# Two image stores cut by channels into uneven pieces, and TensorE's opening put into a loop of one turn, in a Winograd-style 3x3 convolution

## The chip, the cores and the metric

The kernel runs on one core of a Trainium2 chip. The metric is the device time of one execution in microseconds (us); the time before is the median of three runs. The engines are TensorE (PE in the profile, its weight loads PEld), VectorE (DVE), ScalarE (ACT), GpSimd (POOL) and SyncE (SP). Sixteen DMA engines move data between device memory (HBM) and the on-chip memory SBUF. SP, ACT and POOL each issue transfers into a queue of their own (q1, q10 and q0 in the profile, in this order); the sixteen engines serve all three.

## What is computed

A 3x3 convolution with padding of one over 16 images of 64 channels and 64x64 pixels, into 128 output channels, in float32:

```python
batch, c_in, h, w, c_out = 16, 64, 64, 64, 128
x_pad = np.pad(x, ((0, 0), (0, 0), (1, 1), (1, 1)), mode='constant')
...
output[b, co] += weight[co, ci, kh, kw] * x_pad[b, ci, kh:kh+h, kw:kw+w]
```

## The kernel before

**Tiling.** Two images make a pair p (0 to 7): 2 x 64 input channels fill the 128 partitions, so a pair is loaded as one tile of 128 partitions x 64 rows x 64 columns of float32 (2 MB). An output image is one such tile too, with the 128 output channels on the partitions. Eleven such tiles, `homes`, hold inputs and outputs in turn; `IN_HOME` and `OUT_HOME` (L18, L19) say which pair and which image of a pair (b2 = 0 or 1) use which home. A pair is worked on in four blocks of 16 rows, so there are 32 blocks n in all.

**Compute.** For a block, ScalarE casts input rows to fp16 (`cast`, L106), GpSimd adds neighbouring rows (`sums`, L100), TensorE makes three groups of products in PSUM banks (L287), ScalarE copies the first group out of PSUM (L194), and VectorE adds it to the other two into even and odd rows of the output home (L227). TensorE's main loop (L256) has eight turns, one for each pair. Ahead of it stands TensorE's head (L243 to L255): it waits for a tile of zeros, runs seven idle products (`spin(7)`), waits for the weights, transposes them with 18 products, runs four more idle products and gives three credits.

**Transfers.** SP loads the weights, pair 0 in two halves and pairs 1 to 3 (L138 to L142); GpSimd's queue loads pairs 4 to 7 as homes come free (L168, L182). A finished image is stored whole: image b2 = 0 of each pair by SP (L143 to L147), image b2 = 1 by ScalarE's queue (L204 to L209), after VectorE's count for the pair's last block. The last pair alone is stored in two halves of 32 rows. In program counting the pairs start at 0, so the change's "pairs 6 and 7" are p = 5 and p = 6. A store adds 16 to a semaphore: one of its own where the home is used again, else `s_end`. Both (p 5, b2 0) in home 8 and (p 6, b2 0) in home 1 are the last use of their home, so they count on `s_end`. At the end SP waits for 16 times `n_end`, the number of those stores (L299).

**Order.** Every engine's program is written out by hand in issue order; only TensorE loops. A store on SP waits for nothing but VectorE's count, and SP has no other work. The queue of one DMA engine is served in order within SP's, ACT's and POOL's share.

Of the kernel before, what the change touches and what calls it, by code (L numbers as in the profile page):

```python
# [11 lines left out]
H = W = 64  # L12
CO = 128
TILES = 6
G0, G21, G1, G01, G2 = range(5)


IN_HOME = [0, 1, 2, 3, 4, 0, 10, 6]  # L18
OUT_HOME = [(5, 6), (7, 8), (1, 9), (2, 5), (3, 7), (8, 4), (1, 9), (2, 5)]  # L19
CUTS = [(0, 18), (18, 34), (34, 50), (50, 64)]  # L20


def kernel(tc: tile.TileContext, x: bass.AP, weight: bass.AP, out: bass.AP):
    nc = tc.nc
# [3 lines left out]
    def sem(name):  # L28
        return tc.alloc_semaphore(name)

    def sbuf(name, shape, dt):
        return nc.alloc_sbuf_tensor(name, shape, dt).ap()


    s_w, s_pool = sem("s_w"), sem("s_pool")
    s_in = [sem(f"s_in{p}") for p in range(NP)]
    s_in0b = sem("s_in0b")
    s_pe = sem("s_pe")
    s_act = sem("s_act")
    s_dve = sem("s_dve")  # L40
    s_out = {}
    s_end, s_done = sem("s_end"), sem("s_done")
# [14 lines left out]
    PE, ACT, DVE, POOL, SP = nc.tensor, nc.scalar, nc.vector, nc.gpsimd, nc.sync  # L57
# [4 lines left out]
    def free(home):  # L62
        if home not in user:
            return None
        kind, arg = user[home]
        return (s_pe, consumed(arg)) if kind == "in" else (arg, 16)
# [4 lines left out]
    with tc.tile_critical(sync_engine=EngineType.Pool):  # L71
        homes = [sbuf(f"home{k}", [128, H, W], F32) for k in range(11)]
# [4 lines left out]
        w16 = sbuf("w16", [CO, 64 * 9], F16)  # L77
        Wt = sbuf("Wt", [128, 5, 3, CO], F16)
        zeros = sbuf("zeros", [128, 512], F16)
        ident = sbuf("ident", [128, 128], F16)  # L80
        banks = [nc.alloc_psum_tensor(f"bank{k}", [128, RB, W], F32).ap() for k in range(8)]
        flat = [b.rearrange("p j c -> p (j c)") for b in banks]
# [4 lines left out]
        def rows(t):  # L87
            return t.rearrange("p (j i) c -> p j i c", i=2)
# [4 lines left out]
            ).then_inc(s or s_in[p], 16)  # L93

        def store(eng, p, b2, lo, hi, s):
            return eng.dma_start(
                out[2 * p + b2, :, lo:hi, :], homes[OUT_HOME[p][b2]][:, lo:hi, :]
            ).then_inc(s, 16)

        def sums(eng, lo, n, p):  # L100
            v = rows(homes[IN_HOME[p]])
# [4 lines left out]
        def cast(m):  # L106
            lo, hi = CUTS[m % NB]
            return ACT.copy(xs[:, lo:hi, :], homes[IN_HOME[m // NB]][:, lo:hi, :])  # L108
# [3 lines left out]
        pieces, n_end = {}, 0  # L112
        last_user = {}
        for p in range(NP):
            for b2 in range(2):
                last_user[OUT_HOME[p][b2]] = (p, b2)
        for p in range(5):
            user[IN_HOME[p]] = ("in", p)
        for p in range(NP):
            for b2 in range(2):  # L120
                h = OUT_HOME[p][b2]
                gate_out[p, b2] = free(h)
                if last_user[h] == (p, b2):
                    s = s_end
                else:
                    s = s_out[p, b2] = sem(f"s_out{p}{b2}")
                cuts = [(3, 0, H)] if p < NP - 1 else [(1, 0, 32), (3, 32, H)]
                for blk, lo, hi in cuts:
                    pieces[p, b2, blk] = (lo, hi, s)
                    n_end += s is s_end  # L130
                user[h] = ("out", s)
            if p + 5 < NP and p in (0, 1, 2):
                q = p + 5
                gate_in[q] = free(IN_HOME[q])
                user[IN_HOME[q]] = ("in", q)
# [7 lines left out]
        for p in range(NP):  # L143
            for blk in range(NB):
                if (p, 0, blk) in pieces:
                    SP.wait_ge(s_dve, adds(NB * p + blk, 2))
                    store(SP, p, 0, *pieces[p, 0, blk])  # L147
# [5 lines left out]
                out=ident,  # L153
# [17 lines left out]
        for k in range(2, 2 * NP):  # L171
            p = k // 2
# [5 lines left out]
            if k in (4, 6, 8):  # L178
                q = k // 2 + 3
# [5 lines left out]
        wp_bank = {G1: 4, G2: 5, G0: 6}  # L185
# [5 lines left out]
        for n in range(NB * NP):  # L191
            for b2 in range(2):
                when(
                    ACT.copy(uts[n % 2][b2], banks[(6 * n + b2) % 8]), s_pe, tiles(n, 1 + b2)  # L194
                ).then_inc(s_act, 1)
            m = n + 1
            if m < NB * NP:
                if m % NB == 0:
                    ACT.wait_ge(s_in[m // NB], 16)
                if m == 1:  # L200
                    ACT.wait_ge(s_in0b, 16)
                cast(m).then_inc(c_cast, 1)
            done = n - 1
            if done >= 0 and (done // NB, 1, done % NB) in pieces:  # L204
                p = done // NB
                ACT.wait_ge(s_dve, adds(n, 1))
                store(ACT, p, 1, *pieces[p, 1, done % NB])
        ACT.wait_ge(s_dve, adds(NB * NP, 1))
        store(ACT, NP - 1, 1, *pieces[NP - 1, 1, NB - 1])  # L209


# [5 lines left out]
        for n in range(NB * NP):  # L217
            p, blk = divmod(n, NB)
            j0 = RB * blk
            for i in range(2):  # L220
                for b2 in range(2):
                    if blk == 0 and i == 0 and gate_out[p, b2] is not None:
                        DVE.wait_ge(*gate_out[p, b2])
                    if i == 0 and b2 == 0:
                        DVE.wait_ge(s_act, copies(n, 2))
                    add = when(
                        DVE.tensor_add(  # L227
                            rows(homes[OUT_HOME[p][b2]])[:, j0 : j0 + RB, i, :],
                            banks[(6 * n + 2 + 2 * i + b2) % 8],
# [9 lines left out]
        def spin(n):  # L239
            for _ in range(n):  # L240
                PE.matmul(flat[7], zeros[:, 0:128], zeros)  # L241

        PE.wait_ge(s_dve, 1)  # L243
        spin(7)
        PE.wait_ge(s_pool, 3)
        for kh, g in ((1, G1), (2, G2), (0, G0)):
            for k in range(3):
                t = 3 * kh + k
                for q in (0, 64):
                    mm = PE.matmul(  # L250
                        flat[wp_bank[g]][q : q + 64, k * CO : k * CO + CO], w16[:, t::9], ident
                    )
            mm.then_inc(s_pe, 1)
        spin(4)
        PE.sem_inc(c_bank, 3)  # L255
        with nc.Fori(0, NP, engines=(EngineType.PE,), hint_back_edge=True):  # L256
            for blk in range(NB):
# [6 lines left out]
                for gi, (taps, credits) in enumerate(groups):  # L264
# [5 lines left out]
                    for wi, off in taps:  # L270
                        for kw in (1, 0, 2):
                            c_lo, c_hi = max(0, 1 - kw), min(W, W + 1 - kw)
                            for b2 in range(2):
                                p0 = 64 * b2
                                lo, hi = j0, j0 + RB
# [3 lines left out]
                                else:  # L279
# [7 lines left out]
                                mm = PE.matmul(  # L287
                                    acc[b2][:, lo - j0 : hi - j0, c_lo:c_hi],
                                    Wt[p0 : p0 + 64, wi, kw, :],
                                    rhs,  # L290
                                    start=i == 0,
                                    stop=i == n - 1,
                                )
# [36 lines left out]
```

## Time and profile before

| what | us |
|---|---|
| median of 3 runs (128.70 to 128.82) | 128.75 |
| time of the profiled execution | 129.4 |
| span of the profiled execution, first to last instruction | 126.8 |
| VectorE's last add ends (the last work of any compute engine) | 111.7 |
| last store issued | 111.7 |
| SP's wait for the last stores | 14.0 |

The span leaves 2.6 us of the profiled execution's time outside it. The page's strips have 40 slices of 3.17 us each. Its transfers: 17.07 MB read from HBM and 33.55 MB written. Besides its views, the trace keeps one record for each DMA packet (queue, bytes, start, duration) but not the number of the DMA engine that moved it. A packet is one channel's rows of one image or pair: 16,384 bytes for 64 rows, 8,192 for 32.

### The profile page before, as it was taken

Reading aid. Unit: us, or ns where it says so; the run is one execution under the profiler, and the core shown is the slowest. Engines: PE = TensorE matmul, PEld = TensorE weight load, DVE = VectorE, ACT = ScalarE, POOL = GpSimd, SP = SyncE. Lnnn points to the kernel's source line nnn. Section 1 sums busy time; section 2 is a strip of 40 time slices with the busy share of each in tenths; the row PEclk is TensorE's granted clock in tenths of the full one; section 3 lists DMA queues with packets and bytes.
Section 4 is the critical chain, followed back from the end, with each engine's and each line's share of the span. In section 5 each row is a group of like instructions: output and inputs, shape, how many; then the busy total and the mean of one; then the engine's idle time right before and its main releaser. Section 6 shows DMA issues by size and latency. Waiting matters only on the chain.

```text
span 126.8 us, 2528 instructions
## 1 busy us (share of the span) xinstructions
PE 108.3 (85%) x989; PEld 57.2 (45%) x989; DVE 84.1 (66%) x133; ACT 67.2 (53%) x100; POOL 39.1 (31%) x26
## 2 busy tenths in 40 slices
PE   5979999999999999999999999999999999800000
PEld 2535555555555555555555555555555555300000
DVE  0058887888788778777877787778777877720000
ACT  4366656665666566656665666566656666300000
POOL 2218455271517161706060606070707000000000
PEclk9999999999999999999999999999999999997555
DMA  4999999999999999999999999999999999999930
GB/s 125 384 442 450 429 419 424 439 289 413 419 434 450 429 411 424 439 444 419 424 426 444 434 419 419 439 439 429 419 434 429 442 419 419 429 416 434 424 145 13
DMA packets 4035, 50.65 MB, mean 399 GB/s; under 512 B 448, under 2 KB 448, under 8 KB 576
## 3 DMA queue, kind: packets, MB, share of 16 engines
q1 hardware_dynamic: 2160, 25.46, 48.5%
q10 hardware_dynamic: 1296, 16.78, 31.0%
q0 software_dynamic: 576, 8.39, 15.5%
q14 instruction: 3, 0.02, 0.0%
HBM read 17.07 MB, written 33.55 MB: 399 GB/s over the span
## 4 chain that ended last, share of the span: by engine, by line
PE 80%; DVE 1%; DVEq 0%; issue 0%
PE bank L287 80%; DVE home L227 1%; DVEq L71 0%
## 5 line engine op out<-in xcount | busy, mean ns | idle before, releaser
L227 DVE TENSOR_TENSOR home<-bank,ut 128x512 f32<-128x512 f32 x128 | 81.9, 686 | 21.8 <-PE bank L287 21.6
L287 PE MATMUL bank<-xs,Wt 64*128 64x504 f16 (+3 forms) x768 | 87.5, 373 | 0.0
L287 PEld LDWEIGHTS bank<-xs,Wt 64*128 64x128 f16 x768 | 43.9, 94 | 38.2
L194 ACT COPY ut<-bank 128x512 f32<-128x512 f32 x64 | 34.4, 589 | 37.8 <-PE bank L287 37.8
L102 POOL TENSOR_TENSOR ss<-home 128x1024 f16<-128x1024 f32 x15 | 35.5, 2367 | 50.7 <-PE bank L287 48.4
L108 ACT CAST xs<-home 128x1024 f16<-128x1024 f32 (+2 forms) x32 | 33.8, 1058 | 0.0
L287 PE MATMUL bank<-ss,Wt 64*128 64x504 f16 (+1 forms) x192 | 26.5, 377 | 0.7 <-PEq L266 0.7
L287 PEld LDWEIGHTS bank<-ss,Wt 64*128 64x128 f16 x192 | 10.9, 94 | 10.4 <-issue 1.2
L241 PE MATMUL bank<-zeros 128*128 128x512 f16 x11 | 4.5, 567 | 1.4 <-DVE zeros L212 1.4
L91 POOL DMA_DIRECT2D home<-in_x_dram x4 | 2.4, 600 | 4.8 <-DMA home<-in_x_dram 4.8
L213 DVE TENSOR_TENSOR Wt<-Wt 128x384 f16<-128x384 f16 x1 | 0.4, 359 | 4.7 <-ACT Wt L188 4.7
L188 ACT CAST Wt<-bank 128x384 f16<-128x384 f32 x3 | 1.2, 487 | 3.0 <-PE bank L250 3.0
L241 PEld LDWEIGHTS bank<-zeros 128*128 128x128 f16 x11 | 1.3, 131 | 3.3 <-issue 1.7
L188 ACT ACT_TABLE_LOAD x1 | 1.3, 1283 | 0.9 <-PEq L314 0.9
L250 PEld LDWEIGHTS bank<-ident,w 128*64 128x64 f16 x18 | 1.1, 209 | 0.8 <-POOL w L164 0.8
L164 POOL CAST w<-w_raw 128x576 f16<-128x576 f32 x1 | 0.7, 662 | 2.2 <-DMA w_raw<-in_weight_dram 2.2
L250 PE MATMUL bank<-ident,w 128*64 128x128 f16 x18 | 1.3, 327 | 0.0
L102 DVE TENSOR_TENSOR ss<-home 128x512 f16<-128x512 f32 x2 | 1.3, 686 | 0.0
L212 DVE MEMSET zeros<- 128x256 uint32 x1 | 0.3, 272 | 1.1 <-PEq L314 1.1
L214 DVE TENSOR_TENSOR Wt<-Wt 128x384 f16<-128x384 f16 x1 | 0.4, 358 | 0.0
L150 POOL MEMSET ident<- 128x128 f16 x1 | 0.2, 204 | 0.5 <-POOLq L71 0.5
L152 POOL TENSOR_SCALAR_AFFINE_SELECT ident<-ident 128x128 f16<-128x128 f16 x1 | 0.3, 292 | 0.1
(4 smaller groups left out, 0.4 us busy)
## 6 DMA issues: line engine op xcount, KB each, us to landing
out_dram<-home SPq DMA_DIRECT2D x7, 2048.0 KB, 24.1
out_dram<-home ACTq DMA_DIRECT2D x7, 2048.0 KB, 20.3
home<-in_x_dram POOLq DMA_DIRECT2D x4, 2048.0 KB, 20.5
home<-in_x_dram SPq DMA_DIRECT2D x3, 2048.0 KB, 20.8
home<-in_x_dram SPq DMA_DIRECT2D x2, 1024.0 KB, 6.1
out_dram<-home SPq DMA_DIRECT2D x2, 1024.0 KB, 11.7
out_dram<-home ACTq DMA_DIRECT2D x2, 1024.0 KB, 14.0
w_raw<-in_weight_dram SPq DMA_DIRECT2D x1, 288.0 KB, 2.8
```

The source lines that it names most:

```text
L91: return eng.dma_start(homes[IN_HOME[p]][:, lo:hi, :], x_rows[128 * p : 128 * p + 128, lo:hi, :]).then_inc(s or s_in[p], 16)
L102: return eng.tensor_add(ss[:, lo : lo + n, :], v[:, lo : lo + n, 0, :], v[:, lo : lo + n, 1, :])
L108: return ACT.copy(xs[:, lo:hi, :], homes[IN_HOME[m // NB]][:, lo:hi, :])
L164: when(POOL.tensor_copy(w16, w_raw), s_w, 16).then_inc(s_pool, 1)
L188: ACT.copy(wrow(g), flat[wp_bank[g]][:, 0 : 3 * CO]), s_pe, i + 1
L194: ACT.copy(uts[n % 2][b2], banks[(6 * n + b2) % 8]), s_pe, tiles(n, 1 + b2)
L213: when(DVE.tensor_sub(wrow(G21), wrow(G2), wrow(G1)), s_act, 2)
L214: when(DVE.tensor_sub(wrow(G01), wrow(G0), wrow(G1)), s_act, 3)
L227: DVE.tensor_add(rows(homes[OUT_HOME[p][b2]])[:, j0 : j0 + RB, i, :], banks[(6 * n + 2 + 2 * i + b2) % 8], uts[n % 2][b2],),
L241: PE.matmul(flat[7], zeros[:, 0:128], zeros)
L250: mm = PE.matmul(flat[wp_bank[g]][q : q + 64, k * CO : k * CO + CO], w16[:, t::9], ident)
L287: mm = PE.matmul(acc[b2][:, lo - j0 : hi - j0, c_lo:c_hi], Wt[p0 : p0 + 64, wi, kw, :], rhs, start=i == 0, stop=i == n - 1,)
```

## The change

Two things. First, for image 0 of pairs p = 5 and p = 6 SP's one store of 128 channels x 64 rows becomes three: rows 0 to 31 of all channels, then rows 32 to 63 of 120 channels, then rows 32 to 63 of the other eight. The eight are the last ones for p = 5 and the first ones for p = 6. `n_end` counts the added stores. Second, TensorE's head is put, unchanged, into a loop of one turn whose first instruction is placed at slot 0 of a block of instruction fetch; a branch in front of it skips the slots between.

```diff
+PARTS = {
+    (5, 0): [(0, CO, 0, 32), (0, 120, 32, H), (120, CO, 32, H)],
+    (6, 0): [(0, CO, 0, 32), (8, CO, 32, H), (0, 8, 32, H)],
+}
...
         def store(eng, p, b2, lo, hi, s):
-            return eng.dma_start(
-                out[2 * p + b2, :, lo:hi, :], homes[OUT_HOME[p][b2]][:, lo:hi, :]
-            ).then_inc(s, 16)
+            for c0, c1, r0, r1 in PARTS.get((p, b2), [(0, CO, lo, hi)]):
+                eng.dma_start(
+                    out[2 * p + b2, c0:c1, r0:r1, :],
+                    homes[OUT_HOME[p][b2]][c0:c1, r0:r1, :],
+                ).then_inc(s, 16)
...
-                    n_end += s is s_end
+                    if s is s_end:
+                        n_end += len(PARTS.get((p, b2), [0]))
...
-        PE.wait_ge(s_dve, 1)
-        spin(7)
+        with nc.Fori(0, 1, engines=(EngineType.PE,), head_slot={EngineType.PE: 0}):
+            PE.wait_ge(s_dve, 1)
+            spin(7)
...
```

The rest of the head, down to `spin(4)`, moves into the loop with no other edit.

More of the change, by code (lines that the diff above doesn't have):

```diff
@@ L241, in spin @@
                 PE.matmul(flat[7], zeros[:, 0:128], zeros)
-        PE.wait_ge(s_dve, 1)
-        spin(7)
[L245 to L254, printed above, removed]
+        with nc.Fori(0, 1, engines=(EngineType.PE,), head_slot={EngineType.PE: 0}):
+            PE.wait_ge(s_dve, 1)
+            spin(7)
+            PE.wait_ge(s_pool, 3)
+            for kh, g in ((1, G1), (2, G2), (0, G0)):
+                for k in range(3):
+                    t = 3 * kh + k
+                    for q in (0, 64):
+                        mm = PE.matmul(
+                            flat[wp_bank[g]][q : q + 64, k * CO : k * CO + CO], w16[:, t::9], ident
+                        )
+                mm.then_inc(s_pe, 1)
+            spin(4)
         PE.sem_inc(c_bank, 3)
```

## The prediction

> **What bounds the kernel now.** I read the page's strips first, then the chain of waits, then SP's own waits, then the DMA share in short windows at the end.
>
> ```profile
> PE   5979999999999999999999999999999999800000
> PEclk9999999999999999999999999999999999997555
> DMA  4999999999999999999999999999999999999930
> GB/s 125 384 442 450 429 419 424 439 289 413 419 434 450 429 411 424 439 444 419 424 426 444 434 419 419 439 439 429 419 434 429 442 419 419 429 416 434 424 145 13
> ```
>
> The DMA strip is full from the second slice to slice 38 and outlives PE's by four slices. The chain of waits stops where compute ends, and SP's waits show what comes after.
>
> ```profile
> 7.74 101.44 PE bank L287 x948
> 109.18 1.90 DVE home L227 x3
> 111.08 0.60 DVEq L71
> ...
> SPq L299 <- DMA out_dram<-home: 14.0, 1, 14.0
> ```
>
> Compute ends at 111.7; SP then waits 14.0 us (L299) for the last stores. So the transfers set the end. The windows show that it is not all sixteen DMA engines:
>
> ```profile
> 120.00:121.00 1.00, 0.00 (x0) 0.00 (x0) 0.00 (x0) 0.00 (x0) 0.00 (x0) 0.50 1.05 442
> 121.00:122.00 1.00, 0.00 (x0) 0.00 (x0) 0.00 (x0) 0.00 (x0) 0.00 (x0) 0.50 0.43 180
> 122.00:123.00 1.00, 0.00 (x0) 0.00 (x0) 0.00 (x0) 0.00 (x0) 0.00 (x0) 0.50 0.08 33
> 123.00:124.00 1.00, 0.00 (x0) 0.00 (x0) 0.00 (x0) 0.00 (x0) 0.00 (x0) 0.50 0.06 25
> 124.00:125.00 1.00, 0.00 (x0) 0.00 (x0) 0.00 (x0) 0.00 (x0) 0.00 (x0) 0.50 0.08 33
> 125.00:126.80 1.80, 0.00 (x0) 0.00 (x0) 0.00 (x0) 0.00 (x0) 0.00 (x0) 0.50 0.00 0
> ```
>
> The last two columns are the DMA share and GB/s. A share of 1/16 = 0.0625 is one engine: from about 122.3 to 125.3 a single DMA engine works while fifteen stand idle. The packet records (queue, bytes, start and end) say the same to the packet. Each engine's last packet of the two final stores ends between 121.25 and 121.61 on twelve engines, then at 121.91, 121.94, 122.35, and on the last at 125.26; the last landing is at 125.71.
>
> Why is one engine late? A 16,384-byte packet takes 611 ns almost everywhere. One unbroken sequence, each packet starting where the one before ends, does not:
>
> ```
> q10 16384  91.061-91.723  662
> q1  16384  91.720-92.373  653
> q10 16384  92.370-93.014  644
> q1  16384  93.010-93.654  644
> ```
>
> It runs from 28.8 to 113.6, about 130 packets with some 4.0 us over 611 ns in sum, loads among them. Before (9 to 24 us: compute and loads, no stores) no packet exceeds 611; after 113.6 (stores, no compute) its 8,192-byte packets take 309 like the others'. It starts each packet without a gap, so it can finish earlier only if it is given fewer bytes.
>
> **The change, part by part.** *Channels to engines.* A 128-channel store puts 16 completion records, one for each engine, behind 128 data packets: eight packets an engine. The trace shows no 120-channel transfer. Bounds: at eight packets an engine, as now, 120 channels occupy fifteen engines and one is left out; or all sixteen share it and nobody is spared. I take the first as nearest to the rows: one engine then loses eight packets in each of the two images, 16 in all. [...]
>
> *What the spared engine saves.* The last 8,192-byte packets start 0.306 us apart, so 16 x 0.306 = 4.90 us. If it is the late engine it ends at 125.26 - 4.90 = 120.4, and is no longer last.
>
> *What the others pay.* The two eight-channel pieces are 16 packets. At one an engine, eight engines get two more: 2 x 0.306 = 0.61 us (bounds: 0 if the last ones are not among them, and 4.90 if one engine takes all 16). Halving packets costs 2 x 309 - 611 = 7 ns for each of 16 packets, 0.11 us, and a few completion records of 9 ns. So the fifteen end at latest at 122.35 + 0.61 + 0.11 = 123.07, or at 122.46 if the one at 122.35 gets nothing more.
>
> *Conflicts at the source.* In the 128-channel stores each engine reads at 309 ns per 8,192 bytes. Whether fifteen engines reading 120 channels get in each other's way is not in the trace. Bounds: 0, and two engines sharing one path, twice the time: 16 x 0.309 = 4.94 us on every engine. I take 0.3 us, near the lower end: the only slowing seen once transfers run steadily is that late engine's, about 30 ns in 611, and 5% of 4.94 is 0.25.
>
> *SP's added issues.* Four more at 0.332 us. SP issues at 85.5, 98.3 and 104.7 and is idle between, so two more cost 0.66 us of idle time; no one queues behind. Landings here take 10.6 to 29.0 us, the DMA queues being full, so they are hidden; were the queues empty, the later pieces would land up to 0.66 us late, which no step waits for before the end.
>
> *TensorE's head.* It adds a skip to a new fetch block, a register step and a branch, and no product. The nearest rows are PE's 0.7 us behind its sequencer ahead of the main loop, 1.4 us behind the first zeros, and instruction packets of 309 to 436 ns. Bounds: -0.7 to +2 us on the start of the main loop. The loop is 101.4 us with no idle time, so the delay arrives whole at 111.7, and there it is covered by the queue: the last stores, issued at 111.1 and 111.7, would land in about the 6.1 us of the opening 1024-KB loads, at 117.8, if the engines were free, but these are busy to 121.3 at least. That is 3.5 us of cover, and behind the change still some 3 us. Moving it past would cost one for one. I take 0 for the end.
>
> **Sum.** Profiled execution: last packet from 125.26 to between 122.46 and 123.07, a gain of 2.2 to 2.8; less 0.3 for conflicts, 1.9 to 2.5, middle 2.2. From 129.4 this is 127.2. The median of the timed runs is 0.65 lower than the profiled execution: 128.75 - 2.2 = 126.55, say 126.6. Its own range: 125.8 (2.8 and 0.15 of spread) to 128.4 (conflicts of 2 us).
>
> **The rivals.** *Source conflicts decide (slower).* Two engines that read through one path in both 120-channel pieces: 16 packets at 618 instead of 309. The fifteen end at 122.46 + 4.94 = 127.4 or up to 128.0, so 128.75 + 2.1 to 2.7, about 131.1. It breaks even when the extra reaches 2.5 us, that is, when a packet of these pieces averages about 465 ns. For it: the order of channels on engines may change with 120. Against it: loads and stores from two queues mix freely at 611. [...] Chance 0.15.
>
> *Another engine is spared (the change doesn't do what it says).* The late engine keeps its bytes; it ends at 125.26, plus 0.11, plus 0.61 if it is one of the eight: 128.85 to 129.5. The records carry no engine number, which is all that speaks for it. [...] Chance 0.15.
>
> *The lateness belongs to the profiled execution.* The slow packets need compute and stores at once, as records written by the profiler itself would. Then in timed runs all engines end together, and 0.11 to 0.72 is added: 128.9 to 129.5. Against it: the timed median is only 0.65 below the profiled execution, where 3 us of lateness would be missing. Chance 0.13.
>
> *TensorE's head uncovers.* A delay beyond 3 us; say 4 gives back 1 of 2.2: 127.6; a delay over 5.2 makes it slower than before. Chance 0.02, put to that.
>
> **How the numbers follow.** Forecast 0.55. A measurement here can tell about 0.2%, 0.26 us, from no change. The forecast is all faster: 0.55. Of the two rivals at +0.1 to +0.7 (0.28 together), the lowest quarter or so falls within 0.26: same 0.08, slower 0.20. With conflicts 0.15 and the head 0.02, slower is 0.37. The range from 125.8 to 129.5 holds the forecast and these two rivals, 0.83, and leaves out the conflicts' case. The likeliest case alone is 125.8 to 128.4.
>
> **What would show it.** In the changed profile: SP's last wait falls from 14.0 to about 11.5 us; the windows at the end fall from a share near 1 to 0 within about 1.5 us, with no second at 0.06; in the stretch with slow packets, the same engine's sequence is there, 16 packets shorter, and the new 8,192-byte packets take 309 ns. Wrong would be: a lone engine still at the end (the spared one was another), q1 packets of 450 ns and more after 85 us (conflicts), or VectorE's last add later than 114 (the head). If the span falls by 2 us and the timed median does not, the lateness was the profiler's.

## The result and the profile after

The changed kernel takes 133.39 us (median, 132.33 to 133.86) against 128.72 us before, a ratio of 1.035 with a 95% interval of 1.027 to 1.043. A fourth run, at 134.55 us, fell in a slower state of the chip; such runs are left out of the times and ratios here and below. A gain of 2.2 us was forecast; some 4.6 us were lost. The profiled execution after has a span of 132.1 us and a time of 133.86 us.

The page's strips and its packet line, after:

```profile
DMA  4999999999999999999999999999999999999610
GB/s 119 406 442 442 427 437 422 402 318 417 447 412 432 432 429 442 407 442 417 432 434 417 447 407 456 417 437 414 422 439 337 382 375 340 323 392 402 290 79 15
DMA packets 4338, 50.67 MB, mean 384 GB/s; under 512 B 494, under 2 KB 494, under 8 KB 622
```

The DMA strip is still full, so no engine waits for work. But from slice 31 on (a slice is now 3.30 us, so from 99 us) the engines move 323 to 402 GB/s up to slice 37, where they moved 416 to 442 before. Packets under 512 B are the completion records: 494 against 448 before, 46 more. Two stores became two of 128, two of 120 and two of 8 channels, and 46 = 2 x 15 + 2 x 8: the 120 channels do run on fifteen engines and the eight on eight.

The chain of waits and SP's last wait, after:

```profile
8.97 101.44 PE bank L296 x948
110.41 1.90 DVE home L235 x3
112.31 0.60 DVEq L76
```

```profile
SPq L308 <- DMA out_dram<-home: 18.0, 1, 18.0
```

Compute ends 1.2 us later than before (112.9), as the main loop starts at 8.97 instead of 7.74, and SP's wait behind it grows from 14.0 to 18.0 us instead of falling to 11.5. Now the windows from 100 to 120 us, before and then after (the last two columns are DMA share and GB/s):

```profile
100.00:105.00 5.00, 5.00 (x50) 2.64 (x47) 4.33 (x8) 2.63 (x5) 0.00 (x0) 1.00 1.02 434
105.00:110.00 5.00, 5.00 (x51) 2.63 (x46) 3.68 (x7) 2.61 (x5) 0.00 (x0) 1.00 1.02 436
110.00:115.00 5.00, 0.36 (x4) 0.00 (x0) 1.67 (x3) 0.00 (x0) 0.00 (x0) 1.00 0.97 410
115.00:120.00 5.00, 0.00 (x0) 0.00 (x0) 0.00 (x0) 0.00 (x0) 0.00 (x0) 0.55 1.00 424
```

```profile
100.00:105.00 5.00, 5.00 (x50) 2.66 (x48) 3.76 (x7) 3.49 (x6) 0.00 (x0) 1.00 1.03 362
105.00:110.00 5.00, 5.00 (x49) 2.64 (x47) 4.07 (x7) 2.81 (x5) 0.00 (x0) 1.00 0.99 362
110.00:115.00 5.00, 1.60 (x16) 0.68 (x12) 2.50 (x4) 0.18 (x1) 0.00 (x0) 0.92 0.98 328
115.00:120.00 5.00, 0.00 (x0) 0.00 (x0) 0.00 (x0) 0.00 (x0) 0.00 (x0) 0.50 1.00 388
```

Busy all the time, yet slower: that is how packets that hold one another up would show, and the share alone would hide it. The packet records of 100 to 124 us agree: before, every 8,192-byte packet of SP's queue took 309 to 313 ns; after, they take 371 on average and 77 take over 500. The end is ragged too, in the windows after:

```profile
122.00:123.00 1.00, 0.00 (x0) 0.00 (x0) 0.00 (x0) 0.00 (x0) 0.00 (x0) 0.50 1.02 426
124.00:125.00 1.00, 0.00 (x0) 0.00 (x0) 0.00 (x0) 0.00 (x0) 0.00 (x0) 0.50 0.52 221
126.00:127.00 1.00, 0.00 (x0) 0.00 (x0) 0.00 (x0) 0.00 (x0) 0.00 (x0) 0.50 0.21 90
128.00:129.00 1.00, 0.00 (x0) 0.00 (x0) 0.00 (x0) 0.00 (x0) 0.00 (x0) 0.50 0.14 57
129.00:130.00 1.00, 0.00 (x0) 0.00 (x0) 0.00 (x0) 0.00 (x0) 0.00 (x0) 0.50 0.08 33
```

Summing the shares from 120 us on gives the mean end of the sixteen engines: 121.7 before, 125.2 after, 3.5 us later. The last one ends at 130.6 instead of 125.3, 5.3 us later. So some two thirds of the loss fall on all engines, and one third on the last ones alone. The slower packets account for the first part: from 85 us on, the data packets of SP's and ACT's queues take 52 us more in sum than at 611 and 309 ns each, which is 3.2 us for each of the sixteen engines; before, it was 1.7 us in sum.

### The profile page after: what moved, and what is told of

Same layout as the page of the kernel before. It is cut to its first block, busy times and chain, and to the rows that moved or that the text cites. A ratio compares the mean times of both kernels' runs of the same rounds, so it can differ in the third digit from the quotient of the medians.

```text
span 132.1 us, 2536 instructions
## 1 busy us (share of the span) xinstructions
PE 108.0 (82%) x989; PEld 57.1 (43%) x989; DVE 84.2 (64%) x133; ACT 67.2 (51%) x100; POOL 39.0 (30%) x26
## 3 DMA queue, kind: packets, MB, share of 16 engines
q10 hardware_dynamic: 1296, 16.78, 30.6%
## 4 chain that ended last, share of the span: by engine, by line
PE 77%; DVE 1%; DVEq 0%; issue 0%
PE bank L296 77%; DVE home L235 1%; DVEq L76 0%
## 5 line engine op out<-in xcount | busy, mean ns | idle before, releaser
L296 PEld LDWEIGHTS bank<-ss,Wt 64*128 64x128 f16 x192 | 10.9, 94 | 11.5 <-issue 2.3
```

The source lines that it names most:

```text
L296: mm = PE.matmul(acc[b2][:, lo - j0 : hi - j0, c_lo:c_hi], Wt[p0 : p0 + 64, wi, kw, :], rhs, start=i == 0, stop=i == n - 1,)
```

## The experiments

Theory A: the cut pieces make DMA engines meet at the source, that is, wait for each other because they read through the same path. Theory B: TensorE's head holds a DMA engine up. Two questions stood behind them: which engine is the late one, and does the change spare it?

**The change taken apart.** *e1_head_only* has the head in the loop and no cut:

```diff
+PARTS = {}
...
+        with nc.Fori(0, 1, engines=(EngineType.PE,), head_slot={EngineType.PE: 0}):
```

> The kernel before with TensorE's head in the loop of one turn and no cut of the stores. Theory A (conflicts at the source in the 120- and 8-channel pieces make nearly all of the loss): 128.5 to 129.5 us, with compute up to 1.3 us later (ending near 112.9), as in the changed kernel's trace, covered by the DMA queues. Theory B (the head's added 16-KB instruction packet at 3.5 us holds one DMA engine, which stays late to the end): 130 to 131.5 us, with one engine's landings over 1.4 us behind from the first load on.

Measured: ratio 1.0004 (0.997 to 1.004). The chain's last step and SP's last wait:

```profile
112.82 0.60 DVEq L73
```

```profile
SPq L305 <- DMA out_dram<-home: 12.7, 1, 12.7
```

Compute ends at 113.4, 1.7 us later than before, and the wait shrinks by 1.3: the DMA queues cover it, as the prediction said. Not all of the 1.7 us need be the head's: in *e15* below, which has the old head, the main loop starts 1.1 us late too, at 8.87. The records do show the added instruction packet (16,384 bytes, at 4.06 us, 0.93 us long), and a second engine then ends late with the first, at 124.95 instead of about 122 us; it still ends ahead of the late one. Theory B falls.

*e2_parts_only* has the cuts and the old head.

> The kernel before with the two stores cut into 128 x 32 rows, 120 and 8 channels, and TensorE's head as it was. Theory A: 132 to 134 us, packets of the cut pieces well over 309 ns from about 100 us on. Theory B: 127 to 129 us, since without the head's packet the spared engine ends early.

Measured: 133.25 us, ratio 1.039 (1.032 to 1.047). The whole loss is in the cuts.

*e3_rows_only* cuts by rows alone:

```diff
+    (5, 0): [(0, CO, 0, 32), (0, CO, 32, H)],
+    (6, 0): [(0, CO, 0, 32), (0, CO, 32, H)],
```

> The same two stores cut by rows alone, 2 x (128 channels x 32 rows), the head as it was. Theory A: 128.6 to 129.1 us, 8,192-byte packets at 309 ns. If smaller packets or the added issues on SP cost the time: 130 us or more.

Measured: ratio 0.9992 (0.996 to 1.003). Neither smaller packets nor two more issues cost anything. It is the cut by channels.

*e4_112_16* cuts by channels, but into numbers that sixteen engines share evenly:

```diff
+    (5, 0): [(0, CO, 0, 32), (0, 112, 32, H), (112, CO, 32, H)],
+    (6, 0): [(0, CO, 0, 32), (16, CO, 32, H), (0, 16, 32, H)],
```

> The same rows cut into 112 and 16 channels (last sixteen for p = 5, first sixteen for p = 6), the head as it was. Both numbers can be shared evenly by sixteen engines (7 and 1 packets each), so no engine is spared and none gets more. Theory A (any cut off the 128-channel shape makes engines read through the same path): slower by at least 2 us, 131 to 134 us, packets up to 618 ns. If only the uneven load on engines (fifteen, eight) costs: 128.6 to 129.2 us.

Measured: 131.49 us, ratio 1.019 (1.014 to 1.024); 512 completion records, 64 more, so all sixteen engines take part in every piece. Uneven load is not needed for a loss of about 2.4 us. The other half of the loss of 120 and 8 goes with their fewer engines; no run takes their two pieces apart.

**The conflict by itself.** *e5_shapes* has no convolution, only stores:

```diff
+PHASES = [
+    (0, 128, 1), (0, 120, 1), (8, 128, 1), (0, 112, 1), (0, 64, 1),
+    (112, 128, 1), (120, 128, 1), (0, 32, 4), (0, 120, 8),
+]
...
+                SP.dma_start(
+                    out[i, c0:c1:step, 32:H, :], home[c0:c1:step, 32:H, :]
+                ).then_inc(s_phase[k], 16)
```

> No convolution: one SBUF tile of zeros is stored over and over, four stores of 32 rows (8,192 bytes a channel) for each shape, each shape after the one before has landed: channels 0-127, 0-119, 8-127, 0-111, 0-63, 112-127, 120-127, every fourth of 0-31 (8 channels), every eighth of 0-119 (15 channels); at the end 4 x 0-119 from SP beside 4 x 0-127 from ACT. Theory A (conflicts at the source): 128 channels 309 ns a packet, about 10 us for four; both 120s and 112 near 618 ns (18 to 21 us for the 120s), 64 channels near 618, the sixteen and the eight neighbours 1.2 us and more a packet; every fourth channel 309 ns. If uneven load alone costs: 309 ns everywhere, four 120s in the 10 us of four 128s.

It ran once. The windows of its phases, each from its first packet's start to its last one's end, in order: 128 channels, 0-119, 0-111, 0-63, sixteen neighbours, eight neighbours, every fourth of 0-31, and last 0-119 from SP beside 128 from ACT. The columns are window, length, DVE, POOL, PE clock, DMA share, GB/s.

```profile
6.20:16.50 10.30, 0.00 (x0) 0.00 (x0) 1.00 0.98 407
17.60:31.30 13.70, 0.00 (x0) 0.00 (x0) 1.00 0.82 287
...
47.10:58.70 11.60, 0.00 (x0) 0.00 (x0) 1.00 0.91 316
60.20:70.50 10.30, 0.00 (x0) 0.00 (x0) 1.00 0.97 204
71.60:76.90 5.30, 0.00 (x0) 0.00 (x0) 1.00 0.91 99
78.00:83.20 5.20, 0.00 (x0) 0.00 (x0) 1.00 0.47 50
84.80:87.40 2.60, 0.00 (x0) 0.00 (x0) 1.00 0.25 101
...
93.50:124.10 30.60, 0.00 (x0) 0.00 (x0) 1.00 0.83 266
```

The reader is to set the last two columns side by side: 64 channels keep sixteen engines as busy as 128 do, at half the bytes. A packet takes on average:

| channels | ns for 8,192 bytes |
|---|---|
| 0-127 | 316 |
| 0-119 | 375 |
| 8-127 | 376 |
| 0-111 | 377 |
| 0-63 | 623 |
| 112-127 | 1196 |
| 120-127 | 1212 |
| every fourth of 0-31 | 311 |
| every eighth of 0-119 | 491 |

These are about one, two and four times 309 ns, as if one, two or four engines shared a path: eight neighbours (1212 ns) would make four engines meet, while the same number of channels, four apart, would not meet at all (311 ns). The 120s fall short of twice: 334 of their 480 packets still take 309 to 315 ns and the others up to 898. Engines that get out of step would do that; no run shows it. They cost 13.7 us for four where 128 channels cost 10.3. Beside ACT's stores, the case of the kernel, four pieces took 30.6 us to the last engine's end, where twice the 10.3 would be 20.6: 2.5 us a piece, 5.0 for two, an estimate, as no run has 128 channels from both queues. Theory A's 18 to 21 us for the 120s alone was too high; the 4.94 us that the prediction's rival gives for two pieces is close to this.

*e10_sides* asks on which side the engines meet, in SBUF or in HBM, and whether loads suffer too (no convolution either): spaced partitions against neighbouring channels of the output, and the reverse.

```diff
+C8, S8 = slice(0, 8), slice(0, 32, 4)
+PHASES = [
+    ("store", slice(0, 128), slice(0, 128)), ("store", S8, C8), ("store", C8, S8),
+    ("load", slice(0, 128), slice(0, 128)), ("load", slice(0, 64), slice(0, 64)),
+    ("load", S8, C8), ("load", C8, S8),
...
+]
```

> No convolution: four transfers of 32 rows for each case, one case after the other: stores of 128 channels; stores of 8 channels from every fourth partition into neighbouring channels of the output; stores of 8 neighbouring partitions into every fourth channel; loads of 128 channels; loads of 64; loads into every fourth partition; loads into 8 neighbouring partitions; stores of 7 channels 18 apart; stores of 119 channels. Theory A1 (the conflict is on the SBUF side): every-fourth partitions 309 ns whatever the other side, neighbouring partitions about 1,250 ns (4 engines on one path), loads the same as stores, 64 channels about 620. Theory A2 (the conflict is in HBM): the two mixed cases the other way round.

Its windows: stores of spaced partitions into neighbouring channels, stores of neighbouring partitions into spaced channels, and loads of 128 and of 64:

```profile
18.20:20.70 2.50, 0.00 (x0) 0.00 (x0) 1.00 0.26 105
21.80:27.00 5.20, 0.00 (x0) 0.00 (x0) 1.00 0.47 50
28.30:39.60 11.30, 0.00 (x0) 0.00 (x0) 1.00 0.93 371
41.30:51.70 10.40, 0.00 (x0) 0.00 (x0) 1.00 0.95 202
```

Packets took 311 and 1218 ns in the two mixed cases: for stores the SBUF side decides. Loads of 64 channels also run at half the rate (611 ns). The small loads are less clear-cut, 453 ns spaced and 843 neighbouring. In e5 a packet took about twice 309 ns from 64 neighbouring partitions (623, with the DMA share at 0.97) and about four times from eight (1212). What the engines share in SBUF, no run shows.

**Which engine is late.** Three runs add two loads of 8, 15 and 16 channels behind the store of pair 5, into a home that is dead by then. If a transfer on n engines uses the first n of them, the author's assumption, these sets nest, and *first* and *fifth* are meant so below:

```diff
+                    if p == 5:
+                        SP.wait_ge(s_pe, consumed(5))
+                        for i in range(2):
+                            SP.dma_start(
+                                homes[0][i:32:4, :, :], x_rows[128 * i : 128 * i + 128][i:32:4, :, :]
+                            ).then_inc(s_end, 16)
```

> The kernel before and, behind SP's store of pair 5, two more loads of 8 channels x 64 rows into a home that nobody reads any more (16,384 bytes a channel, every fourth partition): two more packets of 611 ns on eight engines. If the late engine is one of those eight: 129.9 to 131.2 us. If not: 128.5 to 129.2 us.

> The same with two loads of 15 channels (every eighth partition): two more packets on fifteen engines. If the late engine is the sixteenth, the one that the change spares: 128.5 to 129.2 us, the others ending 1.2 to 2.4 us later, still ahead of it. If it is one of the fifteen: 129.9 to 131.2 us.

> The control: two loads of 16 channels (every eighth partition), two more packets on all sixteen engines. Whichever engine is late: 129.9 to 131.2 us.

Measured: ratios 1.010 (1.007 to 1.013), 1.009 (1.005 to 1.012) and 1.011 (1.006 to 1.016). The lone engine ends at 126.57, 126.47 and 126.58, each 1.2 to 1.3 us after the 125.26 of before, which is two packets of 0.61. It is among the first eight, so by this order the 120-channel pieces never spared it; it even gets both eight-channel pieces.

*e9_extra7* does the same with 7 channels (`i:28:4`).

> As the run with two added loads of 8 channels, with 7 channels (every fourth partition of 0-27): two more packets on seven engines. In that run eight engines were hit and the late one was among them. If the late engine is the eighth of these (the one that seven-channel transfers leave out): 128.5 to 129.3 us, the lone engine ending near 125.3 as before. If it is one of the first seven: 129.8 to 130.8 us, the lone engine near 126.5.

Measured: 130.75 us, ratio 1.015 (1.012 to 1.018). Its end, from 123 us on:

```profile
123.00:124.00 1.00, 0.00 (x0) 0.00 (x0) 0.00 (x0) 0.00 (x0) 0.00 (x0) 0.50 0.06 25
124.00:125.00 1.00, 0.00 (x0) 0.00 (x0) 0.00 (x0) 0.00 (x0) 0.00 (x0) 0.50 0.06 25
125.00:126.00 1.00, 0.00 (x0) 0.00 (x0) 0.00 (x0) 0.00 (x0) 0.00 (x0) 0.50 0.06 25
126.00:127.00 1.00, 0.00 (x0) 0.00 (x0) 0.00 (x0) 0.00 (x0) 0.00 (x0) 0.50 0.04 16
```

A share of 0.06 to 126.64: still hit, so it is one of the first seven. Two cuts were tried beside it on the guess that it was the eighth.

*e11_sevens*:

```diff
+    (5, 0): [(0, CO, 1, 0, 48)]
+    + [(i, 126, 18, 48, H) for i in range(18)]
+    + [(126, CO, 1, 48, H)],
```

> An attempt at what the change meant, if the late engine is the eighth: the last 16 rows of one image (p = 5, b2 = 0) go out as 18 stores of 7 channels, 18 apart (packets of 4,096 bytes, about 155 ns), and one of 2, so that the late engine loses eight such packets (1.2 us) and seven engines get ten more (1.6 us). 127.6 to 128.4 us if the conflicts stay under 1 us, 128.5 to 130 if they don't or if the late engine is not spared.

*e12_119*:

```diff
+    (5, 0): [(0, CO, 1, 0, 52), (0, 119, 1, 52, H), (119, 126, 1, 52, H), (126, CO, 1, 52, H)],
```

> The same idea in fewer transfers: the last 12 rows of that image as stores of 119, 7 and 2 channels (3,072 bytes, about 118 ns): the late engine loses 0.9 us, seven engines get ten more packets (1.2 us), with conflicts within the 119. 127.9 to 128.6 us if these stay small, 128.7 to 130 if not.

Both lost, at 1.015 (1.013 to 1.018) and 1.012 (1.009 to 1.015). The guess was wrong, but the size fits: the lone engine ends at 126.83 and 126.38, after ten more packets of 0.155 or 0.118 us, 1.6 and 1.2 on top of 125.26.

*e13_stairs* adds loads of 2, 3, 4, 5 and 6 channels, so that each of the first engines gets another number of packets:

```diff
+STAIR = [0, 1, 2, 3, 16, 17]
...
+                        for n in range(2, 7):
+                            c = slice(STAIR[n - 1], STAIR[n - 1] + 4 * n - 3, 4)
+                            SP.dma_start(homes[0][c, :, :], x_rows[0:128][c, :, :]).then_inc(
+                                s_end, 16
+                            )
```

> The kernel before and, behind SP's store of pair 5, five more loads into the dead home, of 2, 3, 4, 5 and 6 channels x 64 rows (16,384 bytes each, every fourth partition). If a transfer of n channels uses the n lowest-numbered engines, the first two engines get five more packets, the next four, three, two, one, and from the seventh on none, at 0.61 us each. The lone engine's last packet, 125.26 before, then names the engine: 128.3 (one of the first two), 127.7 (third), 127.1 (fourth), 126.5 (fifth), 125.9 (sixth), 125.3 (seventh). In time: up to 131.9 us for the first two, 128.9 for the seventh.

Measured: the lone engine ends at 126.69, as late as with two more packets in the four runs above, and its sequence of slow packets in the records holds the same number, 34 of 16,384 bytes in SP's queue behind its last load for POOL, as in e6, e7 and e9. Two steps: the fifth engine. Ten engines' last packets in ACT's queue stay at 121.2 to 121.7, as ten should that get none, so the five loads do nest. In time it is 130.75 us against 129.10, ratio 1.013 (1.008 to 1.018): 1.6 us, for a lone engine that ends 1.4 later.

**The right cut.** By this order only transfers that four engines or fewer share can spare the fifth. *e14_124*:

```diff
+    (5, 0): [(0, CO, 0, 55), (0, 124, 55, H), (124, CO, 55, H)],
```

> The stairs put the late engine fifth. A cut that spares it: the last 9 rows of one image (p = 5, b2 = 0) as stores of 124 channels and of 4, which four engines share (31 and 1 packets of 2,304 bytes, 93 ns in the weights' load). The late engine loses eight packets, 0.74 us; four engines get 24 more, 2.2 us, from 122.4 to 124.6. If no conflict comes with it: 128.2 to 128.6 us, and the lone engine's last packet near 124.5. If conflicts eat it: 128.7 to 129.6 us.

Measured over 12 and 21 runs: 128.47 us against 128.99, ratio 0.9946 (0.991 to 0.998), and a median span of 126.2 us against 126.9. The gain is small, half a per cent, but it beats both kernels. The page's packet line and the windows at its end:

```profile
DMA packets 4172, 50.67 MB, mean 401 GB/s; under 512 B 456, under 2 KB 456, under 8 KB 712
```

```profile
122.00:123.00 1.00, 0.00 (x0) 0.00 (x0) 0.00 (x0) 0.00 (x0) 0.00 (x0) 0.50 0.33 139
123.00:124.00 1.00, 0.00 (x0) 0.00 (x0) 0.00 (x0) 0.00 (x0) 0.00 (x0) 0.50 0.25 106
124.00:125.00 1.00, 0.00 (x0) 0.00 (x0) 0.00 (x0) 0.00 (x0) 0.00 (x0) 0.50 0.06 25
125.00:126.00 1.00, 0.00 (x0) 0.00 (x0) 0.00 (x0) 0.00 (x0) 0.00 (x0) 0.50 0.00 0
```

456 is eight records more than 448: two transfers of four engines. Four engines (0.25) now work to 124, the late one to 124.79, 0.5 us earlier than before, and its sequence holds none of the 2,304-byte packets. Sparing works here, where it spares the right engine and gives four others 24 small packets each.

*e15_one_piece* makes the change's cut in pair 5 alone:

```diff
+    (5, 0): [(0, CO, 0, 32), (0, 120, 32, H), (120, CO, 32, H)],
```

> The change's cut in one image alone (p = 5), the head as it was. Each piece costs 2.9 us beside another queue's stores in the run of shapes, so half of what both pieces cost: 131.0 to 132.0 us. If the loss came from the second piece's place near the end: 128.7 to 129.6 us.

Measured: ratio 1.010 (1.007 to 1.014), 1.3 us, against 5.1 for both pieces: neither bound. On the average engine the pieces do add up: the shares from 120 us on give a mean end of 123.0, against 121.7 before and 124.4 in e2, so 1.3 us for one piece and 2.7 for two. The last engine's end doesn't follow: 126.0 and 129.4, against 125.3 before. That fifteen engines have over 3 us of slack behind the late one, which a first piece can use up and a second can't, would give that shape; no run tells it from the second piece's place near the end.

## Why the prediction was wrong

**What bounds the kernel** was right: the transfers, and among them one late engine. e14 shows that its lateness is worth time in the timed runs too, so the rival that gave it to the profiled execution falls: without it, four engines with 24 more packets each could only have made e14 slower.

**Channels to engines** was right in number (46 more records) and wrong in what it was for. The step that failed first is the clause "if it is the late engine it ends at 125.26 - 4.90 = 120.4". Two loads of 15 channels delay the late engine as two of 8 do (to 126.47 in e7, 126.57 in e6), so it is not the one that fifteen leave out; by the order of e13 it is the fifth. That the two 120-channel pieces leave out the same engine, which then has 16 packets less, was the author's assumption, and no run shows which one they leave out. Nothing in the trace of before told which one was late; the prediction gave that case 0.15.

**Conflicts at the source** is the second failed step, a term sized at 0.3 us. Its bounds were 0 and 4.94, and it was put near the lower end by a row that measures something else, the late engine's 5%. The separate stores give 5.0 us for two pieces beside another queue, and in the changed kernel the slower packets come to 3.2 us on each engine. The rival had this term, and its price of 4.9 us was of the right size; what it left out is that the spared engine might be the wrong one at the same time. The two were priced as alternatives, each from a base in which the other didn't hold. Conflicts alone were put at 131.1; with the late engine not spared either, 128.75 + 4.94 + 0.11 to 0.72 would have given 133.8 to 134.4. That this is near the measured 133.4 is partly luck: the average engine lost less than 4.94 us, and the last one more.

**What the others pay** was off as well: the eight-channel pieces were priced at 0.306 us a packet; eight neighbours stored alone take 1.21 us each (e5), so two would cost 2.4 us and not 0.61. By the loads of e6 the late engine is one of the eight. That fits the ragged end but isn't shown for it: in the changed kernel 24 of SP's 8,192-byte packets take 0.7 to 1.3 us, and the records don't say which piece they belong to.

**Halved packets, SP's issues and TensorE's head** were right: e3 shows nothing for the first two, though with two added issues and not four, and e1 nothing for the head, though compute ends 1.7 us later in its trace. In the changed kernel itself SP's longest issue took 4.0 us instead of 0.33, with nobody waiting behind.

## What to carry to other kernels

Where a kernel is bound by transfers, look at the end by the DMA share in short windows: here a share of one sixteenth (0.06 from 123 to 124 us) was one late engine, and two more packets of 0.61 us on it put the end off by 1.2 to 1.3 us, whether eight engines got them or all sixteen (e6, e8). Before taking bytes off it, find out which engine it is: a few loads of nested sizes into dead memory told it in one run here (e13). A store cut by channels can have a second price: alone, 120 neighbouring channels took 375 ns a packet and 64 took 623, where 128 took 316 and eight spaced ones 311 (e5). Its mark was a busy share near 1 with fewer GB/s, 0.97 and 204 for the 64 against 0.98 and 407 for the 128. When two rivals can both be true, price them together too.

## What the runs showed of the hardware that was not expected

One DMA engine, the fifth by e13, is slow in the trace of before only while compute and stores run together: 611 ns become 615 to 681 for nearly all its 16,384-byte packets from 28.8 to 113.6 us. In e5, with stores of 128 channels and no compute, the sixteen engines end within 0.2 us of each other (16.26 to 16.44), but that is 10 us of one queue alone. Why the engine is slow is open. Eight neighbouring partitions, stored on eight engines, took four times as long a packet as eight spaced ones (1212 against 311 ns in e5). A transfer of fewer channels can use fewer engines: by the completion records it was 15 for 120 channels and 8 for 8 (46 more in the changed kernel), 16 for 112 and 16 (64 more in e4), and 4 for 124 and 4 (8 more in e14).
